# Gate fold, norm sums, first weight sums and final norm of a two-layer decoder trunk: work moved between engines and places

## The chip, the cores and the metric

The kernel runs on one core of a Trainium2 chip. A core has a matrix engine (TensorE, PE in the profile), a vector engine (VectorE, DVE), an activation engine (ScalarE, ACT), a general engine (GpSimd, POOL), and a queue engine (SyncE, SP) that issues most of the transfers. The metric is the device time of one execution in microseconds (us).

## The reference

The model is a trunk of two layers on 1024 tokens of width 1024, in float32. Cut to what matters here:

```
def rmsnorm(x, g):
    y = x * rsqrt(mean(x * x, -1) + EPS)
    return y * g

# layer 0
h = rmsnorm(x, g_mix[0])
x = x + gla_layer_mix(h, mem_k, mem_v, ...)        # gated linear attention beside memory attention
x = x + conv_ffn(rmsnorm(x, g_ffn[0]), w_up[0], conv_w[0], conv_b[0], w_down[0])
# keys and values of sparse attention, made once
shared = nsa_shared_kv(x, g_kv, w_kv, ...)
# layer 1
h = rmsnorm(x, g_mix[1])
q, gl, mq = split_cols(h @ w_in, [512, 24, 512])
gates = sigmoid(gl)                                # 24 per token: 8 heads x 3 branches
m = mem_attend(mq, mem_k, mem_v)                   # 4 heads over 256 memory tokens
x = x + concat(nsa_attend(q, gates, *shared), m) @ w_out
x = x + conv_ffn(rmsnorm(x, g_ffn[1]), w_up[1], ...)
return rmsnorm(x, g_final)

def conv_ffn(h, w_up, conv_w, conv_b, w_down):
    a, b = split(h @ w_up, 2)                      # w_up: 1024 x 5632, so 22 tiles of 128 columns each
    a = causal conv of width 3 over time(a) + conv_b
    return (silu(a) * b) @ w_down
```

## The kernel before

Activations lie transposed: 8 tiles `xs[k]` of 128 features by 1024 tokens, worked in two halves of 512 tokens. TensorE takes a float32 product as three passes over values split in two: a rounded high part and the rest (low part), high x high, high x low, low x high. So each operand is split first: ScalarE copies the high part (`Ah`, line 979), VectorE subtracts it from the source for the low part (`Al`, line 980). The program is recorded in the order of the Python code, generators woven by weights, and a list scheduler then sets each engine's order from the dependences and its own costs; buffers come from pools by tag (`U` gives 128x512 buffers, `V` 128x1024).

**Feed-forward, up part.** Each layer has 22 units (`Up`), one for each tile of columns. A unit loads its weights (`load`, two tiles `wu` of 128x1024), and makes seven products p1 to p7 of combined weights with combined activations `B[1]` to `B[7]` (a seven-product scheme in place of eight). p1 and p2 need the raw weights; p6 and p7 (PSUM tile `fy`), p3 and p5 (`fw`) need sums of them, which `sums()` makes in place by four 128x512 operations at lines 999 to 1002, all on GpSimd; then `split67` and `split35` split them. The list `seq` begins with the units us[0] and us[1] (worked as a pair), then us[6], us[2] and so on. The combined activations come from `blocks0` and `blocks1` (lines 553 to 586 are their VectorE operations), behind the norm of the attention's result. While VectorE is at that, ScalarE and VectorE also split the raw weights of the first units (`pre`, `direct`).

**Norms.** `Norm.add` squares a tile on ScalarE (`nsq`, line 256) and adds it into one of two running sums `nacc` (line 266): the first sum on GpSimd, the second on VectorE, in the output projections of the two attention stages (`out_proj`); all on VectorE elsewhere. `done` adds the two sums (line 274), lets TensorE sum over the features (`ms`, line 278), and calls `inv_rms`: logarithm and exponential on ScalarE give a first value y of the inverse root, and one Newton step of four VectorE operations (lines 241 to 244) refines it, y(1.5 - 0.5 (ms + eps) y y).

**Gates.** In layer 1, `front` makes the keys to be compressed (`comp_in`, for each of two kinds one VectorE operation, eight ScalarE copies `ck`, and in the second half two additions at line 1465) and the 24 gates of each token (`gsb`, line 1479) for one half of the tokens after the other. High and low contributions of a gate stand in two rows, so eight small matmuls with a 0/1 matrix `fold` (`gateT`, line 1497) add them and turn them to tokens; three small operations (lines 1499 to 1501, tile `ope`) start the sigmoid. This stands ahead of the memory attention: `mkv.project()` (TensorE `mk`, lines 192 to 194, over four weights whose low parts are `wmkl`, line 177, and then the sums `mms`, line 353), and with it `compress()` (`hid`, line 1536).

**End.** The down part of the feed-forward (`dn`, lines 1341 to 1343) adds its products to `x` on VectorE (line 1389, or line 1306 when it leaves PSUM into scaled sums). In layer 1 its output comes in three segments: 512 tokens, 256, 256 (the third and fourth quarters). For each, `finish` takes the norm and scales 8 tiles with the gain and the inverse root: six by one VectorE operation (line 1830), two (k = 1 and 4) by GpSimd (line 1827) and ScalarE (line 1828), and stores two or four tiles at a time (SyncE). `after_ffn1` weaves the three `finish` generators with what is left of the down part (`d`).

The lines that set the order around the change:

```
weave((front(0), 14.0), (second, 9.0))          # gates and compressed keys of the first half
drain(front(1))                                  # of the second half
... fold, gateT, ope                             # lines 1492 to 1501
weave((mem_all(), 107.0), (compress(), 15.0))

def after_ffn1(d, nn, segs):
    drain(take(d, 5))
    weave((finish(segs[0], nn[0]), 9.0), (take(d, 10), 27.0))
    drain(take(d, 4 + 4))
    weave((finish(segs[1], nn[1]), 9.0), (take(d, 4), 3.6))
    drain(finish(segs[2], nn[2]))
```

Of the kernel before, what the change touches and what calls it, by code (L numbers as in the profile page):

```python
# [10 lines left out]
AF = mybir.ActivationFunctionType  # L11
# [3 lines left out]
P = 128  # L15
# [3 lines left out]
HT = 512  # L19
# [15 lines left out]
def kernel(  # L35
# [46 lines left out]
    def PS(s="ps"):  # L82
        return pp.tile([P, HT], F32, tag="ps", name=nm(s))
# [22 lines left out]
    def weave(*gens):  # L106
        drain(blend(*gens))
# [43 lines left out]
    def col(c):  # L151
        return cs[:, c : c + 1]
# [83 lines left out]
    def inv_rms(ms, n, y=None, a=None):  # L236
        y = U(s="rs") if y is None else y
        a = U(s="rt") if a is None else a
        nc.scalar.activation(a[:, :n], ms, AF.Ln, bias=epsc)
        nc.scalar.activation(y[:, :n], a[:, :n], AF.Exp, scale=-0.5)  # L240
        nc.vector.scalar_tensor_tensor(a[:, :n], ms, EPS, y[:, :n], ALU.add, ALU.mult)
        nc.vector.tensor_tensor(a[:, :n], a[:, :n], y[:, :n], ALU.mult)
        nc.vector.tensor_scalar(a[:, :n], a[:, :n], -0.5, 1.5, ALU.mult, ALU.add)
        nc.vector.tensor_tensor(y[:, :n], y[:, :n], a[:, :n], ALU.mult)
        return y

    class Norm:
        def __init__(self, width=HT, pool=True):
            self.eng = (nc.gpsimd if pool else nc.vector, nc.vector)
            self.acc = [None, None]  # L250
            self.n = 0
            self.w = width
# [6 lines left out]
        def add(self, xt):  # L259
            j = self.n % 2  # L260
            self.n += 1
            if self.acc[j] is None:
                self.acc[j] = self.square(xt, "nacc")
            else:
                sq = self.square(xt, "nsq")
                self.eng[j].tensor_tensor(self.acc[j], self.acc[j], sq, ALU.add)

        def add_last(self, xt):
            self.acc.append(self.square(xt, "nsq"))
# [335 lines left out]
    def mix_a():  # L605
# [3 lines left out]
        last_x = [None]  # L609

        def stats(half, h=None):
            n = Norm(pool=False)
            tvs = []
            for k2 in range(4):
                t = V(s="x0")
# [324 lines left out]
    def ffn(l, blocks_, after):  # L940
        B, rest = blocks_
        segs = [(0, HT), (HT, HT)]
        ends = segs if l == 0 else [(0, HT), (HT, HT // 2), (HT + HT // 2, HT // 2)]
        nn = [Norm(w, False) for _, w in ends]
        silu = [None]

        ring = {}
# [18 lines left out]
        class Up:  # L966
# [28 lines left out]

            def sums(self):
                (a0, b0), (a1, b1) = ((t[:, hs(0)], t[:, hs(1)]) for t in self.raw)
                tt = nc.gpsimd.tensor_tensor
                tt(b1, b0, b1, ALU.add)  # L999
                tt(b0, a0, b0, ALU.subtract)  # L1000
                tt(a0, b1, a0, ALU.subtract)
                tt(a1, a1, a0, ALU.subtract)
# [124 lines left out]
        def each(group, *whats):  # L1127
            for what in whats:
                for u in group:
                    getattr(u, what)()  # L1130
# [37 lines left out]
        seq = pair + order[:-1]  # L1168
        for n, u in enumerate(seq):
            u.n, u.mate = n // 2, seq[n - 1] if n % 2 else None  # L1170
        each(pair, "load", "direct")
        each(pair, "p1")
        pair[0].p2()
# [258 lines left out]
    def mix_b(second, h, rs, rst):  # L1432
# [58 lines left out]
        fold = cp.tile([64, 24], F32, name="fold")  # L1491
        nc.vector.tensor_tensor(fold, ident[0:64, 0:24], ident[0:64, 32:56], ALU.add)
        ope = cp.tile([P, 8, 24], F32, name="ope")
        pg = PS("gateT")
        for qt in range(8):
            t = gsb[qt // 4][0:64, (qt % 4) * P : (qt % 4 + 1) * P]
            mm(pg[:, qt * 24 : (qt + 1) * 24], t, fold, start=True, stop=True)
        opf = ope.rearrange("p a b -> p (a b)")
        nc.vector.tensor_scalar(opf, pg[:, :192], -87.0, None, ALU.max)
        nc.scalar.activation(opf, opf, AF.Exp, scale=-1.0)  # L1500
        nc.vector.tensor_scalar(opf, opf, 1.0, None, ALU.add)

        hid = [S([P, 2, P], s="state", bufs=2) for i in range(2)]

        rows = [slice(0, 64), slice(64, 128)]
# [45 lines left out]
            yield from att.rest()  # L1551

        weave((mem_all(), 107.0), (compress(), 15.0))

        kcr = [S([P, 2, P], F32R, s="state", bufs=2) for _ in range(2)]
        vc = S([P, P], s="vcmp", bufs=1)
# [257 lines left out]
            weave(*gens)  # L1814
        return second_half(op0, b_wo, x_d, nn, C_FFN + 8)

    def finish(seg, nrm):
        t0, w = seg
        rs = nrm.done()[:, :w]
        per = 2 * HT // w  # L1820
        for k in range(KT):
            if k % per == 0:
                o = V(s="fin")
            ov = o[:, (k % per) * w : (k % per + 1) * w]
            xv = xs[k][:, t0 : t0 + w]
            if k in (1, 4):
                nc.gpsimd.tensor_tensor(ov, xv, rs, ALU.mult)
                nc.scalar.activation(ov, ov, AF.Copy, scale=col(C_FIN + k))
            else:
                nc.vector.scalar_tensor_tensor(ov, xv, col(C_FIN + k), rs, ALU.mult, ALU.mult)  # L1830
            if k % per == per - 1:
                nc.sync.dma_start(
                    out[k + 1 - per : k + 1, :, t0 : t0 + w].rearrange("k p t -> p k t"),
                    o[:, : per * w].rearrange("p (k t) -> p k t", k=per),
                )
            yield 1.0

    def after_ffn1(d, nn, segs):
        drain(take(d, 5))
        weave((finish(segs[0], nn[0]), 9.0), (take(d, 10), 27.0))  # L1840
        drain(take(d, 4 + 4))
        weave((finish(segs[1], nn[1]), 9.0), (take(d, 4), 3.6))
        drain(finish(segs[2], nn[2]))

    b = ffn(0, mix_a(), after_ffn0)
    ffn(1, mix_b(*b), after_ffn1)
# [102 lines left out]
```

## Time and profile before

| what | value |
|---|---|
| three timed runs | 2336.86, 2341.9, 2342.29 us; median 2341.9 us |
| profiled execution | 2342.82 us, of which the span is 2341.0 us |
| mean granted clock of TensorE in it | 0.991 of full speed |
| TensorE busy | 2264.1 us, 97% |
| VectorE busy | 1743.6 us, 74% |
| ScalarE busy | 1130.0 us, 48% |
| GpSimd busy | 442.2 us, 19% |

The profiled execution is 1.8 us longer than its span: that much lies around the span. TensorE's matmuls are pipelined, so one is shown longer (0.39 us for 128x512) than the step from one start to the next. A granted clock of 0.50 is the lower of the two levels of TensorE's clock, 1.2 GHz, and 1.00 the higher, 2.4 GHz. The names of buffers in the rows stand without their numbers; `fy<-B,Ah` is a matmul from activations `B` and high parts `Ah` into `fy`.

### The profile page before, as it was taken

The numbers are of one execution on the slowest core, as the hardware profiler recorded it, in microseconds if no ns is written. First come the engines' busy times: TensorE is split into PE (matmuls) and PEld (weight loads), VectorE is DVE, ScalarE is ACT, GpSimd is POOL, SyncE is SP. The second block draws the span as 40 slices with busy tenths as digits, with TensorE's granted clock in tenths as the row PEclk, the third lists the DMA queues.
The fourth block names the chain that finished last, engine by engine and source line by source line (L and its number), as shares of the span: only waits on it lengthen the run. The fifth ranks groups of instructions, "written<-read, shape, count | busy, mean of one in ns | idle before, by whom it ended". The sixth has DMA issues, their size and how long they took to land.

```text
span 2341.0 us, 31315 instructions
## 1 busy us (share of the span) xinstructions
PE 2264.1 (97%) x11062; PEld 1842.3 (79%) x11062; DVE 1743.6 (74%) x3065; ACT 1130.0 (48%) x2054; POOL 442.2 (19%) x383
## 2 busy tenths in 40 slices
PE   8999999999999999999899999999999999999997
PEld 6888777777888888788787877767777788888886
DVE  6785876977876668886656688884978777768876
ACT  5463454533333335456444688773543333335454
POOL 1211301323333200000002121110323422210001
PEclk9999999999999999999999999999999999999999
DMA  6233146433432329542421111027434433229533
GB/s 216 93 109 101 54 144 202 135 112 122 140 122 95 108 98 330 167 131 105 126 89 37 45 44 35 8 61 225 136 108 135 140 104 108 95 87 338 165 96 102
DMA packets 138892, 284.94 MB, mean 122 GB/s; under 512 B 16086, under 2 KB 22403, under 8 KB 138736
## 3 DMA queue, kind: packets, MB, share of 16 engines
q1 hardware_dynamic: 130144, 262.20, 34.4%
q0 software_dynamic: 3840, 12.24, 1.5%
q10 hardware_dynamic: 4752, 8.51, 1.0%
q8 instruction: 86, 1.41, 0.3%
q14 instruction: 70, 0.57, 0.1%
HBM read 211.06 MB, written 71.83 MB: 121 GB/s over the span
## 4 chain that ended last, share of the span: by engine, by line
PE 75%; DVE 13%; DMA 4%; ACT 3%; issue 3%; POOL 1%; SPq 1%; DVEq 0%; POOLq 0%; ACTq 0%
PE dn L1342 5%; PE dn L1341 5%; PE dn L1343 5%; PE fy L1017 5%; PE fy L1015 4%; PE fy L1016 4%; PE no L1753 3%; PE fw L1017 3%; PE fw L1016 3%; PE fw L1015 3%; PE npt L1737 2%; PE fx L1015 2%; PE fx L1016 2%; PE fx L1017 2%; PE sc L1680 2%
## 5 line engine op out<-in xcount | busy, mean ns | idle before, releaser
L1341 PE MATMUL dn<-db,da 128*128 128x512 f32 (+1 forms) x628 | 242.8, 387 | 2.1 <-DVE x L1306 2.1
L1342 PE MATMUL dn<-db,da 128*128 128x512 f32 (+1 forms) x628 | 242.6, 387 | 1.0 <-DVE db L1271 1.0
L1343 PE MATMUL dn<-db,da 128*128 128x512 f32 (+1 forms) x628 | 242.2, 386 | 0.0
L1015 PE MATMUL fy<-B,Ah 128*128 128x512 f32 x496 | 197.0, 397 | 16.7 <-DVE q L1049 8.7
L1017 PE MATMUL fy<-B,Al 128*128 128x512 f32 x496 | 195.9, 395 | 1.7 <-DVE Al L980 1.4
L1016 PE MATMUL fy<-B,Ah 128*128 128x512 f32 x496 | 195.3, 394 | 0.0
L979 ACT ACTIVATE Ah<-wu 128x1024 fp32r<-128x1024 f32 x124 | 130.3, 1052 | 106.6 <-PE fy L1016 61.7
L980 DVE TENSOR_TENSOR Al<-wu,Ah 128x1024 fp32r<-128x1024 f32 x124 | 161.6, 1304 | 20.8 <-ACT Ah L979 20.8
L999 POOL TENSOR_TENSOR wu<-wu,wu 128x512 f32<-128x512 f32 x44 | 61.3, 1394 | 558.7 <-DVE Al L980 320.6
L1341 PEld LDWEIGHTS dn<-db,da 128*128 128x128 f32 x628 | 118.1, 188 | 26.6 <-issue 2.8
L1342 PEld LDWEIGHTS dn<-db,da 128*128 128x128 f32 x628 | 118.0, 188 | 26.2 <-DVE db L1271 2.8
L1017 PE MATMUL fw<-B,Al 128*128 128x512 f32 x352 | 137.9, 392 | 0.0
L1016 PE MATMUL fw<-B,Ah 128*128 128x512 f32 x352 | 137.2, 390 | 0.0
L1015 PE MATMUL fw<-B,Ah 128*128 128x512 f32 x352 | 137.1, 390 | 0.0
L1343 PEld LDWEIGHTS dn<-db,da 128*128 128x128 f32 x628 | 118.0, 188 | 23.5
L1271 DVE TENSOR_TENSOR db<-bl,db 128x512 fp32r<-128x512 f32 x154 | 107.6, 699 | 31.3 <-ACT db L1270 30.4
L1015 PEld LDWEIGHTS fy<-B,Ah 128*128 128x128 f32 x496 | 94.2, 190 | 41.8 <-DVE q L1049 12.9
L1017 PEld LDWEIGHTS fy<-B,Al 128*128 128x128 f32 x496 | 94.2, 190 | 23.8 <-DVE Al L980 4.0
L1270 ACT ACTIVATE db<-bl 128x512 fp32r<-128x512 f32 x154 | 95.6, 622 | 30.3 <-PE dn L1343 21.8
L1016 PEld LDWEIGHTS fy<-B,Ah 128*128 128x128 f32 x496 | 94.3, 190 | 19.2
L192 PE MATMUL op<-om,wor 128*128 128x512 f32 x256 | 103.0, 404 | 1.9 <-ACT om L224 1.9
L1270 ACT ACTIVATE da<-wb 128x512 fp32r<-128x512 f32 x88 | 55.1, 629 | 98.4 <-PE dn L1342 61.3
(424 smaller groups left out, 6239.6 us busy)
## 6 DMA issues: line engine op xcount, KB each, us to landing
wu<-in_w_up_dram SPq DMA_DIRECT2D x176, 256.0 KB, 3.0
bl<-gb_d SPq DMA_DIRECT2D x154, 256.0 KB, 2.8
gb_d<-fc SPq DMA_DIRECT2D x132, 256.0 KB, 3.0
wb<-in_w_down_dram SPq DMA_DIRECT2D x44, 256.0 KB, 4.6
wa<-in_w_down_dram SPq DMA_DIRECT2D x22, 512.0 KB, 7.8
wo<-in_a_wo_dram SPq DMA_DIRECT2D x16, 512.0 KB, 3.7
xre<-om_d SPq DMA_DIRECT2D x32, 256.0 KB, 5.1
x_r<-x SPq DMA_DIRECT2D x32, 256.0 KB, 2.4
```

The source lines that it names most:

```text
L192: mm(ps, wr[:, k, :], hr, start=(k == 0), stop=False)
L979: a = nc.scalar.activation(hi, src, AF.Copy)
L980: b = nc.vector.tensor_tensor(lo, src, f(hi), ALU.subtract)
L1015: mm(ps, wr, hr, start=(first and j == 0), stop=False, skip_group_check=True)
L1016: mm(ps, wr, hl, start=False, stop=False, skip_group_check=True)
L1017: mm(ps, wl, hr, start=False, stop=(stop and j == 3), skip_group_check=True)
L1270: nc.scalar.activation(w[:, hs(0)], t, AF.Copy)
L1271: b = tt(w[:, hs(1)], t, f(w)[:, hs(0)], ALU.subtract)
L1341: mm(o, hi, bh, start=first, stop=False, skip_group_check=True)
L1342: mm(o, hi, bl, start=False, stop=False, skip_group_check=True)
L1343: mm(o, lo, bh, start=False, stop=stop or n == NP - 1, skip_group_check=True)
L1753: mm(acc[a * 64 : a * 64 + 64, :256], v, pf[:, a * 256 : (a + 1) * 256], start=(n == 0), stop=(n == last[a]),)
```

## The change

1. `inv_rms`: y y comes from a ScalarE `Square`; VectorE has three operations in place of four.
2. `Norm.add`: every addition is on VectorE.
3. `sums()` of the first four units of each layer (us[0], us[1], us[6], us[2]) is on VectorE, that of the other 18 stays on GpSimd.
4. The gates' fold with its three small operations is recorded behind the memory attention and `compress`, ahead of the compressed keys' product.
5. `finish` gets the inverse root as an argument; the 512-token segment is scaled by VectorE alone; in the two quarters ScalarE multiplies by the gain, which doesn't need the norm, and VectorE multiplies four tiles at a time by the inverse root. `after_ffn1` takes the norms of both quarters before either is scaled.

```diff
@@ inv_rms
-        nc.vector.scalar_tensor_tensor(a[:, :n], ms, EPS, y[:, :n], ALU.add, ALU.mult)
-        nc.vector.tensor_tensor(a[:, :n], a[:, :n], y[:, :n], ALU.mult)
+        nc.scalar.activation(a[:, :n], y[:, :n], AF.Square)
+        nc.vector.scalar_tensor_tensor(a[:, :n], ms, EPS, a[:, :n], ALU.add, ALU.mult)
         nc.vector.tensor_scalar(a[:, :n], a[:, :n], -0.5, 1.5, ALU.mult, ALU.add)
         nc.vector.tensor_tensor(y[:, :n], y[:, :n], a[:, :n], ALU.mult)
@@ Norm.add
-                self.eng[j].tensor_tensor(self.acc[j], self.acc[j], sq, ALU.add)
+                nc.vector.tensor_tensor(self.acc[j], self.acc[j], sq, ALU.add)
@@ Up.sums
-                tt = nc.gpsimd.tensor_tensor
+                tt = (nc.vector if self.soon else nc.gpsimd).tensor_tensor
@@ ffn
             u.n, u.mate = n // 2, seq[n - 1] if n % 2 else None
+            u.soon = n < 4
@@ mix_b
-        pg = PS("gateT")
-        for qt in range(8):
...
-        nc.vector.tensor_scalar(opf, opf, 1.0, None, ALU.add)
-
         hid = [S([P, 2, P], s="state", bufs=2) for i in range(2)]
...
         weave((mem_all(), 107.0), (compress(), 15.0))
+
+        pg = PS("gateT")
+        for qt in range(8):
+            t = gsb[qt // 4][0:64, (qt % 4) * P : (qt % 4 + 1) * P]
+            mm(pg[:, qt * 24 : (qt + 1) * 24], t, fold, start=True, stop=True)
+        opf = ope.rearrange("p a b -> p (a b)")
+        nc.vector.tensor_scalar(opf, pg[:, :192], -87.0, None, ALU.max)
+        nc.scalar.activation(opf, opf, AF.Exp, scale=-1.0)
+        nc.vector.tensor_scalar(opf, opf, 1.0, None, ALU.add)
@@ finish, after_ffn1
-    def finish(seg, nrm):
+    def finish(seg, rs):
         t0, w = seg
-        rs = nrm.done()[:, :w]
...
-            if k in (1, 4):
-                nc.gpsimd.tensor_tensor(ov, xv, rs, ALU.mult)
-                nc.scalar.activation(ov, ov, AF.Copy, scale=col(C_FIN + k))
+            if per == 2:
+                nc.vector.scalar_tensor_tensor(ov, xv, col(C_FIN + k), rs, ALU.mult, ALU.mult)
             else:
-                nc.vector.scalar_tensor_tensor(ov, xv, col(C_FIN + k), rs, ALU.mult, ALU.mult)
+                nc.scalar.activation(ov, xv, AF.Copy, scale=col(C_FIN + k))
             if k % per == per - 1:
+                o3 = o.rearrange("p (k t) -> p k t", k=per)
+                if per > 2:
+                    nc.vector.tensor_tensor(o3, o3, rs.unsqueeze(1).broadcast_to([P, per, w]), ALU.mult)
...
     def after_ffn1(d, nn, segs):
-        drain(take(d, 5))
-        weave((finish(segs[0], nn[0]), 9.0), (take(d, 10), 27.0))
-        drain(take(d, 4 + 4))
-        weave((finish(segs[1], nn[1]), 9.0), (take(d, 4), 3.6))
-        drain(finish(segs[2], nn[2]))
+        drain(take(d, 11))
+
+        def first():
+            yield from finish(segs[0], nn[0].done())
+
+        weave((first(), 9.0), (take(d, 8), 21.6))
+        drain(take(d, 4 + 3))
+        r1 = nn[1].done()[:, : segs[1][1]]
+        drain(d)
+        r2 = nn[2].done()[:, : segs[2][1]]
+        drain(finish(segs[1], r1))
+        drain(finish(segs[2], r2))
```

What this does to the order is shown at three places.

GpSimd before, at the sums of the third and fourth unit of layer 0 (us[6] has the tiles `wu_3507` and `wu_3508`, us[2] `wu_3505` and `wu_3506`):

```order
L999 TENSOR_TENSOR wu_3506<-wu_3505,wu_3506 128x512
L1000 TENSOR_TENSOR wu_3505<-wu_3505 128x512
L1001 TENSOR_TENSOR wu_3505<-wu_3506,wu_3505 128x512
L1002 TENSOR_TENSOR wu_3506<-wu_3506,wu_3505 128x512
L999 TENSOR_TENSOR wu_3508<-wu_3507,wu_3508 128x512
L1000 TENSOR_TENSOR wu_3507<-wu_3507 128x512
L1001 TENSOR_TENSOR wu_3507<-wu_3508,wu_3507 128x512
L1002 TENSOR_TENSOR wu_3508<-wu_3508,wu_3507 128x512
```

VectorE before, in the same stretch; `Al_3809` is the low part that the third unit's p6 needs:

```order
L1064 TENSOR_TENSOR fc_3575<-fc_3575,s_648_3544 128x512
L980 TENSOR_TENSOR Al_3524<-wu_3508,Ah_3523 128x1024
L1063 TENSOR_TENSOR s_650_3559<-fy_3831,s_650_3559 128x512
L1064 TENSOR_TENSOR fc_3604<-fc_3604,s_650_3559 128x512
L1069 TENSOR_TENSOR q_3829<-fw_3900,q_3829 128x512
L980 TENSOR_TENSOR Al_3809<-wu_3507,Ah_3808 128x1024
L1069 TENSOR_TENSOR q_3844<-fw_3914,q_3844 128x512
L980 TENSOR_TENSOR A_3518<-wu_3507,A_3518 128x512
```

VectorE in the changed kernel, in the same stretch:

```order
L1062 TENSOR_TENSOR s_650_3559<-fy_3831,s_650_3559 128x512
L998 TENSOR_TENSOR wu_3508<-wu_3507,wu_3508 128x512
L1063 TENSOR_TENSOR fc_3604<-fc_3604,s_650_3559 128x512
L999 TENSOR_TENSOR wu_3507<-wu_3507 128x512
L1068 TENSOR_TENSOR q_3829<-fw_3900,q_3829 128x512
L1000 TENSOR_TENSOR wu_3507<-wu_3508,wu_3507 128x512
L998 TENSOR_TENSOR wu_3506<-wu_3505,wu_3506 128x512
L1001 TENSOR_TENSOR wu_3508<-wu_3508,wu_3507 128x512
L979 TENSOR_TENSOR Al_3809<-wu_3507,Ah_3808 128x1024
L1068 TENSOR_TENSOR q_3844<-fw_3914,q_3844 128x512
L999 TENSOR_TENSOR wu_3505<-wu_3505 128x512
L1000 TENSOR_TENSOR wu_3505<-wu_3506,wu_3505 128x512
```

The eight sums have gone from GpSimd to VectorE, and those of the third unit, which stood behind those of the fourth, now stand ahead of three of them; the low part `Al_3809` comes after five sums.

TensorE before, at the gates' fold (`gsb_8390` holds the gates of the first half of the tokens, `gsb_8538` those of the second; the `mk` around are those of the first memory weight):

```order
L193 MATMUL mk_8579<-mh_8432,wmkr_8580 128x256
L194 MATMUL mk_8579<-mh_8432,wmkl_8581 128x256
L1497 MATMUL gateT_8557<-fold,gsb_8538 128x24 x4
L192 MATMUL mk_8579<-mh_8437,wmkr_8580 128x256
L193 MATMUL mk_8579<-mh_8437,wmkr_8580 128x256
L194 MATMUL mk_8579<-mh_8437,wmkl_8581 128x256
```

TensorE in the changed kernel, in the same place; the first weight's `mk` run without a break:

```order
L192 MATMUL mk_8567<-mh_8432,wmkr_8568 128x256
L193 MATMUL mk_8567<-mh_8432,wmkr_8568 128x256
L194 MATMUL mk_8567<-mh_8432,wmkl_8569 128x256
L192 MATMUL mk_8567<-mh_8437,wmkr_8568 128x256
L193 MATMUL mk_8567<-mh_8437,wmkr_8568 128x256
```

TensorE in the changed kernel, some 640 rows later, where the fold now stands:

```order
L472 MATMUL mo_9732<-mpT_9721,mV_8805 128x512
L1549 MATMUL gateT_9742<-fold,gsb_8390 128x24 x4
L1549 MATMUL gateT_9742<-fold,gsb_8538 128x24 x2
L473 MATMUL mo_9732<-mpT_9721,mV_8805 128x512
L471 MATMUL mo_9732<-mpT_9729,mV_8808 128x512
L472 MATMUL mo_9732<-mpT_9729,mV_8808 128x512
L473 MATMUL mo_9732<-mpT_9729,mV_8808 128x512
L1549 MATMUL gateT_9742<-fold,gsb_8538 128x24 x2
```

The fold of the second half no longer stands between the `mk` of the first weight; both halves' fold stands among the last products of the memory attention (`mo`) and ahead of the compressed keys' product.

VectorE before, at the end of the program (the four `x` tiles of the last quarter's second block are done one by one; `rs_18975` is the third quarter's inverse root, `rs_19052` the fourth's):

```order
L1389 TENSOR_TENSOR x_17731<-dn_18518,x_17731 128x256
L1830 SCALAR_TENSOR_TENSOR fin_18983<-x_17727,cs,rs_18975 128x256
L1830 SCALAR_TENSOR_TENSOR fin_18983<-x_17731,cs,rs_18975 128x256
L266 TENSOR_TENSOR nacc_18755<-nacc_18755,nsq_19011 128x256
L1830 SCALAR_TENSOR_TENSOR fin_18983<-x_17733,cs,rs_18975 128x256
L266 TENSOR_TENSOR nacc_18747<-nacc_18747,nsq_19029 128x256
L1830 SCALAR_TENSOR_TENSOR fin_19016<-x_17497,cs,rs_18975 128x256
L1830 SCALAR_TENSOR_TENSOR fin_19016<-x_17499,cs,rs_18975 128x256
L1830 SCALAR_TENSOR_TENSOR fin_19016<-x_17501,cs,rs_18975 128x256
L1389 TENSOR_TENSOR x_17733<-dn_18519,x_17733 128x256
L241 SCALAR_TENSOR_TENSOR rt_19053<-ms_19048,rs_19052 128x256
L242 TENSOR_TENSOR rt_19053<-rt_19053,rs_19052 128x256
```

VectorE in the changed kernel, at the end:

```order
L265 TENSOR_TENSOR nacc_18724<-nacc_18724,nsq_19005 128x256
L1389 TENSOR_TENSOR x_17733<-dn_18519,x_17733 128x256
L242 SCALAR_TENSOR_TENSOR rt_19013<-ms_19008,rt_19013 128x256
L243 TENSOR_SCALAR rt_19013<-rt_19013 128x256
L244 TENSOR_TENSOR rs_19012<-rs_19012,rt_19013 128x256
L1832 TENSOR_TENSOR fin_19044<-fin_19044,rs_19012 128x1024
L242 SCALAR_TENSOR_TENSOR rt_19037<-ms_19032,rt_19037 128x256
L1832 TENSOR_TENSOR fin_19051<-fin_19051,rs_19012 128x1024
L243 TENSOR_SCALAR rt_19037<-rt_19037 128x256
L244 TENSOR_TENSOR rs_19036<-rs_19036,rt_19037 128x256
L1832 TENSOR_TENSOR fin_19058<-fin_19058,rs_19036 128x1024
L1832 TENSOR_TENSOR fin_19065<-fin_19065,rs_19036 128x1024
```

The scalings of the third quarter stood ahead of the last addition to `x`; now every addition stands ahead of them, the fourth quarter's norm is refined between them, and there are four scalings of 128x1024 in place of 12 of 128x256.

## Rows read from the trace of the kernel before

**Rows 1.** The page, part 1: busy time, share and instructions of each engine.

```profile
PE 2264.1 (97%) x11062; PEld 1842.3 (79%) x11062; DVE 1743.6 (74%) x3065; ACT 1130.0 (48%) x2054; POOL 442.2 (19%) x383
```

**Rows 2.** TensorE's waits: releaser; us in total, times, longest us.

```profile
PE gateT L1497 <- DVE gsb L1479: 8.2, 1, 8.2
PE fy L1015 <- ACT Ah L979: 8.0, 4, 4.0
...
PE gr L194 <- DVE wrl L177: 2.5, 1, 2.5
...
PE ms L278 <- DVE nacc L274: 2.2, 2, 1.3
...
PE dn L1341 <- DVE x L1306: 2.1, 1, 2.1
```

**Rows 3.** Windows: us, PE, PEld, DVE, ACT, POOL busy; PEclk, DMA, GB/s.

```profile
504.00:506.00 2.00, 1.88 (x5) 0.97 (x5) 1.48 (x2) 0.00 (x0) 0.00 (x0) 0.50 0.08 9
...
1130.00:1132.00 2.00, 2.00 (x14) 2.00 (x13) 1.21 (x4) 1.06 (x1) 0.00 (x0) 0.65 0.50 90
...
80.00:100.00 20.00, 17.51 (x96) 14.86 (x95) 18.57 (x21) 11.26 (x14) 7.26 (x4) 1.00 0.24 69
440.00:460.00 20.00, 18.50 (x78) 14.42 (x78) 19.82 (x28) 10.13 (x17) 5.73 (x4) 1.00 0.24 89
```

**Rows 4.** TensorE's timeline at the third unit: start, us, instruction, idle before.

```profile
503.59 0.80 PE L1015 MATMUL fy<-B,Ah 128*128 128x512 f32 x1 [3.97 <-ACT Ah L979]
...
510.20 0.39 PE L1017 MATMUL fx<-B,Al 128*128 128x512 f32 x1
...
1742.76 0.80 PE L1015 MATMUL fy<-B,Ah 128*128 128x512 f32 x1 [3.57 <-ACT Ah L979]
```

**Rows 5.** Timeline of GpSimd and ScalarE ahead of it.

```profile
491.56 1.67 POOL L999 TENSOR_TENSOR wu<-wu,wu 128x512 f32<-128x512 f32 x1 [45.59 <-DVE A L980]
...
501.19 1.26 POOL L1001 TENSOR_TENSOR wu<-wu,wu 128x512 f32<-128x512 f32 x1
...
502.48 1.06 ACT L979 ACTIVATE Ah<-wu 128x1024 fp32r<-128x1024 f32 x1 [10.78 <-POOL wu L1001]
```

**Rows 6.** VectorE's timeline at the start of the feed-forward, layer 0.

```profile
427.95 1.22 DVE L980 TENSOR_TENSOR Al<-wu,Ah 128x1024 fp32r<-128x1024 f32 x1
...
437.77 1.78 DVE L266 TENSOR_TENSOR nacc<-nacc,nsq 128x512 f32<-128x512 f32 x1
...
463.39 2.49 DVE L225 TENSOR_TENSOR B<-x,B 128x512 fp32r<-128x512 f32 x4
```

**Rows 7.** VectorE's lines from 426 to 447 us: busy us, mean ns, idle before.

```profile
L980 DVE TENSOR_TENSOR Al<-wa,Ah 128x1024 fp32r<-128x1024 f32 x4 | 8.1, 2033 | 2.4 <-ACT Ah L979 2.4
```

**Rows 8.** Timeline of three engines at the gates' fold.

```profile
1092.27 0.91 ACT L227 ACTIVATE mh<-mem,cs 128x256 fp32r<-128x256 f32 x2 [3.67 <-DMA mem<-in_mem_dram]
...
1125.93 1.90 PE L1497 MATMUL gateT<-fold,gsb 64*128 64x24 f32 x8 [8.17 <-DVE gsb L1479]
...
1128.75 1.22 DVE L177 TENSOR_TENSOR wmkl<-wmk,wmkr 128x1024 fp32r<-128x1024 f32 x1
...
1138.46 0.59 PE L353 MATMUL mms<-macc,on_d 128*128 128x256 f32 x2
```

**Rows 9.** Timeline of the end.

```profile
2283.36 3.50 POOL L1827 TENSOR_TENSOR fin<-x,rs 128x512 f32<-128x512 f32 x2 [206.18 <-DVE rs L244]
...
2324.55 0.28 PE L1342 MATMUL dn<-db,da 128*128 128x256 f32 x1
2324.67 0.28 PE L1343 MATMUL dn<-db,da 128*128 128x256 f32 x1
2327.45 1.13 PE L278 MATMUL ms<-nacc,on_d 128*128 128x256 f32 x4 [2.50 <-DVE nacc L266]
...
2328.50 0.41 DVE L1389 TENSOR_TENSOR x<-dn,x 128x256 f32<-128x256 f32 x1
...
2333.32 3.40 DVE L1830 SCALAR_TENSOR_TENSOR fin<-x,cs,rs 128x256 f32<-128x256 f32 x6
```

More of the change, by code (lines that the diff above doesn't have):

```diff
@@ L247, with __init__ @@
     class Norm:
-        def __init__(self, width=HT, pool=True):
-            self.eng = (nc.gpsimd if pool else nc.vector, nc.vector)
+        def __init__(self, width=HT):
             self.acc = [None, None]
@@ L611, in stats @@
         def stats(half, h=None):
-            n = Norm(pool=False)
+            n = Norm()
             tvs = []
@@ L943, in ffn @@
         ends = segs if l == 0 else [(0, HT), (HT, HT // 2), (HT + HT // 2, HT // 2)]
-        nn = [Norm(w, False) for _, w in ends]
+        nn = [Norm(w) for _, w in ends]
         silu = [None]
@@ L1493, in mix_b @@
         ope = cp.tile([P, 8, 24], F32, name="ope")
-        pg = PS("gateT")
-        for qt in range(8):
[L1496 to L1500, printed above, removed]
-        nc.vector.tensor_scalar(opf, opf, 1.0, None, ALU.add)
         hid = [S([P, 2, P], s="state", bufs=2) for i in range(2)]
@@ L1825, in finish @@
             xv = xs[k][:, t0 : t0 + w]
-            if k in (1, 4):
-                nc.gpsimd.tensor_tensor(ov, xv, rs, ALU.mult)
-                nc.scalar.activation(ov, ov, AF.Copy, scale=col(C_FIN + k))
+            if per == 2:
+                nc.vector.scalar_tensor_tensor(ov, xv, col(C_FIN + k), rs, ALU.mult, ALU.mult)
             else:
-                nc.vector.scalar_tensor_tensor(ov, xv, col(C_FIN + k), rs, ALU.mult, ALU.mult)
+                nc.scalar.activation(ov, xv, AF.Copy, scale=col(C_FIN + k))
             if k % per == per - 1:
[L1832 to L1835, printed above, removed]
+                o3 = o.rearrange("p (k t) -> p k t", k=per)
+                if per > 2:
+                    nc.vector.tensor_tensor(o3, o3, rs.unsqueeze(1).broadcast_to([P, per, w]), ALU.mult)
+                nc.sync.dma_start(out[k + 1 - per : k + 1, :, t0 : t0 + w].rearrange("k p t -> p k t"), o3)
             yield 1.0
     def after_ffn1(d, nn, segs):
-        drain(take(d, 5))
-        weave((finish(segs[0], nn[0]), 9.0), (take(d, 10), 27.0))
-        drain(take(d, 4 + 4))
-        weave((finish(segs[1], nn[1]), 9.0), (take(d, 4), 3.6))
-        drain(finish(segs[2], nn[2]))
+        drain(take(d, 11))
[8 more added lines that the diff above has]
+        drain(finish(segs[2], r2))
     b = ffn(0, mix_a(), after_ffn0)
```

## The prediction

> **What bounds the kernel now.** The page comes first: TensorE is busy 97% of the span, so about 77 us of the whole are its idle time, and VectorE follows at 74% [rows 1]. A change on the other engines can therefore only give back waits of TensorE, or what a wait costs behind its end; 0.3% is 7 us, about what a measurement of this kernel can tell from no change. So the next view is TensorE's waits, and there I look for the lines that the diff touches. Five of them are there: the gates' fold waits 8.2 us in one piece, p6 waits 8.0 us for the high parts `Ah`, the norm's matmul 2.2 us for the sums of squares, the down product 2.1 us for `x` [rows 2], and the last norm 2.5 us [rows 9].
>
> The third view is the windows, for the granted clock. The two p6 waits are 3.97 and 3.57 us [rows 4], and behind the first the clock stands at 0.50, 1.2 GHz; behind the fold's wait it is 0.65 as late as 1130 to 1132 [rows 3]. Where TensorE waited 2.5 us for another low part (`gr` [rows 2], between 80 and 100 us) the clock stayed at 1.00 [rows 3]. So the long waits cost twice. Between the p6 at 503.59 and the matmul at 510.20 there are 14 matmuls; at the full clock they step by 0.227 us, 3.2 us in all, and they took 6.6: 3.4 us lost [rows 4]. I take the same for layer 1.
>
> **A, the fold.** Removed are 8.2 us of waiting and the low clock from 1125.93 to about 1131.4 (0.65 in the last window is 1.4 us of two at half rate), 5.5 us at half rate, 2.7 us lost. But something else is late next. Ahead of the sums `mms` TensorE needs the low part of the third memory weight, which VectorE began at 1128.75 and had at 1129.97 [rows 8]. In the changed order the compressed keys' copies stand ahead of the memory's on ScalarE, which idled 3.67 us for the memory's transfer at 1092 [rows 8]; I estimate that the second half's chain (norm, keys, third weight) moves up by 2 to 3 us through that and through the three small operations that are gone, so the third low part is there at 1127.0. TensorE, no longer held, has 24 `mk`, 16 `hid` and 24 more `mk` from 1115.1 on, 0.12 us each as the steps of that size at the end [rows 9], some 7.9 us: it arrives at 1123.0 and waits 4.0. Then 24 more, and `mms` begins at 1130.7 if the clock holds, at 1132.3 if it falls, in place of 1138.46 [rows 8]: 7.8 or 6.2 us. The fold itself is paid later, at most 1.1 us (the eight small matmuls; the first four ran ahead without a wait). I take 6. Bounds: if the third weight is no earlier, 3; if the fold hides in a wait of the memory attention and the clock holds, 8.
>
> The Trainium skill's page "TensorE: Matmul & The Clock Gate", Part 1, says that the throttled clock is the default and activity releases it. By that the new 4 us of idle time would bring the low clock back, and A would be the 6.2 less 1.1; the trace agrees at 3.57 and 3.97 us of waiting. The sum does not hang on it, as 5.1 lies inside the bounds above.
>
> **B, the start of both feed-forwards.** The third unit's p6 waited since GpSimd did the fourth unit's sums first: it began at 491.56 and reached the third unit's third sum at 501.19, and ScalarE's `Ah` followed at 502.48 [rows 5]. In the new order VectorE does the third unit's sums first. A 128x512 operation of two tensors takes it 0.62 us (2.49 over four [rows 6]). From 491.4 it has two low parts (1.8 us), three operations on TensorE's results and three sums (3.7 us), so ScalarE can begin `Ah` near 497 and has it by 498.9 at the latest, ahead of TensorE's arrival at 499.6 (503.59 less 3.97 [rows 4]). Both p6 waits go, with their low clock: 3.97 + 3.57 + 2 x 3.4 = 14.3 us.
>
> VectorE pays eight sums more (5.0 us) and about three additions of squares (1.9 us) in the stretch from 426 to 469, where it is already full: 19.82 of 20 us [rows 3]. One Newton operation, 0.7, goes. Against these 6.2 us stands what GpSimd's presence costs it now: four low parts there took 8.1 us [rows 7] where an undisturbed one takes 1.22 [rows 6], 3.2 us too much; the addition at 437.77 took 1.78 in place of 0.62 [rows 6], and three more operations lose 0.8 each by my estimate, 6.8 in all. So the stretch comes out even or 0.6 shorter, and the norm's wait of 2.2 us [rows 2] goes with the slow additions. That makes 14.3 + 2.2 = 16.5; I take off 0.5 for waits of a few tenths that move: 16. Bounds: 17.5 if small waits for the low parts go as well, 8 if VectorE is the late one at p6 and the clock falls all the same, so that only part of the wait and the 2.2 come back.
>
> **C, the down product.** Its 2.1 us wait for `x` [rows 2] lies where GpSimd's scaling of the first segment (two operations, 3.50 us at 2283.36 [rows 9]) runs beside VectorE. The scaling now starts later in the down part, and GpSimd has none. I take 1.9; bounds 0 and 2.1.
>
> **D, the end.** The last matmul begins at 2324.67, but the last addition to `x` only at 2328.50, behind the third quarter's scalings; from there to the end of the span are 12.5 us [rows 9]. In the new order nothing of that stands ahead of it. ScalarE is the limit then: 16 gain copies and the squares, some 0.42 each by my estimate, and the last square is about 2.2 us earlier than it was. Behind it the norm has one ScalarE operation more and one VectorE operation fewer (even), and the last six scalings of 3.40 us [rows 9] become two of 1.2, one of the third quarter's ahead of the last ones: 0.2 better. I take 2.4, bounds 0.5 (ScalarE's queue eats it) and 4 (all of the 3.5 us that the addition waited, and the shorter scalings).
>
> **E, small losses.** Every norm has a `Square` more on ScalarE, in layer 0's feed-forward behind a table load; 12 additions of squares come to VectorE; the two gate tiles hold 2 of 14 buffers through the memory attention. I take 1.3 us of loss in all, bounds 0 and 4; cover is ScalarE's half-idle time and VectorE's quarter [rows 1].
>
> **Sum.** 6 + 16 + 1.9 + 2.4 - 1.3 = 25.0 us off the profiled execution of 2342.8 gives 2317.8. The median of the runs is 0.9 below the profiled one, so the forecast is 2317.
>
> **Rivals.** *More comes back* (2310): every term at its upper bound, 8 + 17.5 + 2.1 + 4 and no loss, is 31.6. For it: VectorE without GpSimd beside it may be ahead everywhere. Against it: A has a new wait whose end I can name.
>
> *The waits at p6 change their name* (2329): VectorE, with five sums ahead of `Al`, is late at p6 by 2 to 4 us, and the low clock stays. Then B is 8 and E doubles to 2.6 while C and D hold: 6 + 8 + 1.9 + 2.4 - 2.6 = 15.7, or 2326; with A at its lower bound, 2329. For it: 19.82 of 20 us [rows 3]. Against it: VectorE is idle ahead of p6 now, and the sums fit there.
>
> *Nothing comes of it* (2340): each wait removed meets one that is as late, as a transfer of weights behind the sums would be. Against it: `Ah` waited 10.78 us for GpSimd's sum and for nothing else [rows 5].
>
> *Slower* (2350): VectorE's long durations at 426 to 447 are its own and not GpSimd's doing. Then 6.2 us come on top of a full engine in each layer, the activations `B` are late by as much, and TensorE waits 6 us at p6 and runs at half rate for 3.4 more, twice: 18.8 us lost, the third unit's 14.3 us not gained, and A, C and D give 10.3 back: 8.5 slower. It decides from about 2 us of backlog per layer on, if the clock falls with it. Against it: the same low part takes 1.22 and 2.03 within the one stretch [rows 6, 7], and GpSimd's own sums took 1.67 beside VectorE and 1.26 when that was idle [rows 5].
>
> **Chances.** The forecast with A to E inside their bounds, 2311 to 2325, has 0.60; more comes back 0.15; the waits change their name 0.15; nothing 0.06; slower 0.04. The range from 2308 to 2333 takes in the first three with little of the edges lost. All three are faster by over 0.3%, less 0.02 for a weak third case: 0.88. Within 0.3% 0.07, slower 0.05 with 0.01 for mishaps in E.
>
> **What would show it.** In the changed profile the `fy` line has no wait over 1 us for `Ah`, and the clock is 1.00 behind the third unit's p6 in both layers; `gateT` waits for nothing; a new wait of 3 to 5 us stands at `mk` for `wmkl` near 1123 to 1127; the low parts at the start of the feed-forward take 1.2 us each; the last addition to `x` follows the last matmul within 1 us. The prediction is wrong if the windows behind p6 still show 0.50, if VectorE's stretch from the attention's end to the third unit has grown, or if the last square starts no earlier behind the last matmul than 4 us.

## The result

| | us |
|---|---|
| kernel before, six runs | 2336.86 to 2343.62, median 2340.22 |
| changed kernel, six runs | 2315.2 to 2322.32, median 2318.12 |
| forecast, range | 2317, 2308 to 2333 |
| ratio, 95% interval | 0.9902, 0.9887 to 0.9917 |
| profiled executions: spans | 2341.0 before, 2313.7 after |

The kernel became faster by 22.1 us in the medians, 0.9%, where 25 were forecast. The sum held; its terms did not hold alike. The profiled execution of before is one of its longer ones and that of after one of the shorter, so the two traces lie 27.3 us apart.

### The profile page after: what moved, and what is told of

It reads as the page before. It is cut to its first block, busy times and chain, and to the rows that moved or that the text cites. A ratio compares the mean times of both kernels' runs of the same rounds, so it can differ in the third digit from the quotient of the medians.

```text
span 2313.7 us, 31260 instructions
## 1 busy us (share of the span) xinstructions
PE 2256.4 (98%) x11062; PEld 1839.1 (79%) x11062; DVE 1735.4 (75%) x3086; ACT 1139.0 (49%) x2081; POOL 365.4 (16%) x333
## 3 DMA queue, kind: packets, MB, share of 16 engines
q8 instruction: 87, 1.43, 0.3%
## 4 chain that ended last, share of the span: by engine, by line
PE 84%; DVE 7%; DMA 4%; ACT 3%; issue 2%; SPq 1%; POOL 0%; DVEq 0%; ACTq 0%; POOLq 0%
PE dn L1342 5%; PE dn L1341 5%; PE dn L1343 5%; PE fy L1014 5%; PE fy L1016 4%; PE fy L1015 4%; PE fx L1014 3%; PE no L1753 3%; PE fx L1015 3%; PE fx L1016 3%; PE fw L1016 3%; PE fw L1015 3%; PE fw L1014 3%; PE npt L1737 2%; PE op L193 2%; PE op L192 2%
## 5 line engine op out<-in xcount | busy, mean ns | idle before, releaser
L978 ACT ACTIVATE Ah<-wu 128x1024 fp32r<-128x1024 f32 x124 | 130.4, 1052 | 100.9 <-PE fy L1015 60.3
L998 POOL TENSOR_TENSOR wu<-wu,wu 128x512 f32<-128x512 f32 x36 | 49.3, 1369 | 744.4 <-DVE Al L979 410.6
L1014 PEld LDWEIGHTS fy<-B,Ah 128*128 128x128 f32 x496 | 93.4, 188 | 36.3 <-DVE q L1048 10.4
```

The costliest lines, as they stand in the source:

```text
L978: a = nc.scalar.activation(hi, src, AF.Copy)
L1014: mm(ps, wr, hr, start=(first and j == 0), stop=False, skip_group_check=True)
```

## The profile after

The first view is again the page, then TensorE's waits (releaser; us in total, times, longest us).

```profile
PE 2256.4 (98%) x11062; PEld 1839.1 (79%) x11062; DVE 1735.4 (75%) x3086; ACT 1139.0 (49%) x2081; POOL 365.4 (16%) x333
```

```profile
PE fy L1014 <- DVE q L1048: 6.6, 7, 1.4
PE mk L194 <- DVE wmkl L177: 5.0, 1, 5.0
PE fy L1014 <- ACT Ah L978: 4.7, 3, 2.7
```

The reader is to see what is gone and what is new. The lines of `gateT`, of `ms` for VectorE's sums and of `dn` for `x` [rows 2] are gone. The line of `fy` for `Ah` has fallen from 8.0 to 4.7 us only, and a line of 5.0 us for `wmkl` has come. The line of `fy` for `q`, VectorE's operation on the result of a unit's p6, was 8.7 us before and is 6.6; no part of the change is aimed at it.

**At the third unit** ScalarE's timeline now reads:

```profile
497.73 1.06 ACT L978 ACTIVATE Ah<-wu 128x1024 fp32r<-128x1024 f32 x1 [6.48 <-DVE wu L1000]
```

`Ah` starts at 497.73 in place of 502.48 [rows 5]; p6 starts at 499.96 without a wait in place of 503.59 [rows 4]. The windows of after (us, PE, PEld, DVE, ACT, POOL busy, PEclk, DMA, GB/s) show the clock behind it, in layer 0 and in layer 1, and then a place where it did fall:

```profile
500.00:502.00 2.00, 2.00 (x10) 1.65 (x9) 1.94 (x4) 1.55 (x2) 0.00 (x0) 1.00 0.45 120
...
1726.00:1728.00 2.00, 2.00 (x10) 1.65 (x10) 1.74 (x3) 1.37 (x3) 0.00 (x0) 1.00 0.79 262
...
514.00:516.00 2.00, 2.00 (x7) 1.56 (x7) 2.00 (x5) 0.63 (x1) 0.00 (x0) 0.62 0.00 0
516.00:518.00 2.00, 2.00 (x7) 1.57 (x6) 2.00 (x4) 0.00 (x0) 0.00 (x0) 0.53 0.49 137
```

The low clock of 0.50 at p6 is gone [rows 3]. In layer 0 the next unit's p6 waits. Its `Ah` on ScalarE stands behind the split of the weights of the unit after it, and that one waits for those weights, whose transfer (first row, from SyncE's timeline) was issued only behind VectorE's low part of 504.55 to 505.77, the last to read that buffer:

```profile
506.21 0.42 SPq L975 DMA_DIRECT2D wu<-in_w_up_dram  x1
...
510.63 1.06 ACT L978 ACTIVATE Ah<-wu 128x1024 fp32r<-128x1024 f32 x1 [2.77 <-DMA wu<-in_w_up_dram]
...
513.72 0.50 PE L1014 MATMUL fy<-B,Ah 128*128 128x512 f32 x1 [2.72 <-ACT Ah L978]
```

In the kernel before, the same split at 514.90 waited for nothing: TensorE was up to 7 us later there, and ScalarE came to this split behind other work. This is a wait that the prediction did not have; in layer 1 it is 1.1 us.

**At the start of the feed-forward** VectorE's low parts are no longer stretched (line; busy us, mean ns; idle before), where the mean was 2033 ns [rows 7]:

```profile
L979 DVE TENSOR_TENSOR Al<-wa,Ah 128x1024 fp32r<-128x1024 f32 x4 | 4.9, 1220 | 2.2 <-ACT Ah L978 2.2
```

**At the gates' old place** TensorE no longer waits for `gsb`, but for the third memory weight; its row, and those of VectorE ahead of it:

```profile
1121.54 1.22 DVE L1465 TENSOR_TENSOR ck<-ck,pe 128x1024 f32<-128x1024 f32 x1 [0.81 <-ACT ck L1459]
...
1123.01 1.22 DVE L177 TENSOR_TENSOR wmkl<-wmk,wmkr 128x1024 fp32r<-128x1024 f32 x1
...
1124.29 0.58 PE L194 MATMUL mk<-mh,wmkl 128*128 128x256 f32 x1 [4.99 <-DVE wmkl L177]
```

The low part's source on ScalarE had been ready since 1114.3; VectorE came to it at 1123.01 because two additions `ck` stood ahead of it in its order and waited for ScalarE's copies. The clock fell to 0.50 again (0.51 from 1122 to 1124); `mms` starts at 1129.02.

**At the fold's new place**, ahead of the compressed keys' product `kcmp`, the fold's matmuls now take time of TensorE that is not idle otherwise, the row below and 0.62 us more from 1255.13 on (the trace has two records for each of the eight):

```profile
1252.57 1.51 PE L1549 MATMUL gateT<-fold,gsb 64*128 64x24 f32 x12
```

**At the end**, from the last matmul of the down part on:

```profile
2300.68 0.28 PE L1343 MATMUL dn<-db,da 128*128 128x256 f32 x1
...
2301.00 0.42 DVE L1389 TENSOR_TENSOR x<-dn,x 128x256 f32<-128x256 f32 x1 [1.03 <-PE dn L1343]
...
2302.45 0.70 PE L277 MATMUL ms<-nsq,on_d 128*128 128x256 f32 x2 [0.62 <-ACT nsq L255]
```

The last addition follows the last matmul after 0.3 us, where it took 3.8 [rows 9]; from that matmul to the end of the span are 13.0 us in place of 16.3.

Where the time went is best seen by stage. The borders are the first starts of matmuls into named tiles (`op` of the second half of the tokens, the norm `ms` behind the first feed-forward, `mms`, `kcmp`, which is the compressed keys' product, `fx` and `dn` of the second feed-forward), read off each trace; the table has the time between them in us.

| execution | feed-forward 0 | to `mms` | to `kcmp` | sparse attention | feed-forward 1 up | down and end |
|---|---|---|---|---|---|---|
| before | 682.4 | 64.3 | 124.9 | 408.2 | 438.2 | 231.2 |
| after | 678.3 | 58.4 | 126.7 | 405.0 | 427.8 | 225.3 |
| the whole change again (below) | 675.4 | 58.0 | 129.3 | 405.4 | 427.5 | 225.5 |
| the fold alone | 684.3 | 60.3 | 128.0 | 407.7 | 435.5 | 233.0 |
| the sums alone | 672.3 | 64.2 | 124.0 | 406.8 | 430.4 | 231.7 |
| the end alone | 681.8 | 63.7 | 123.9 | 406.0 | 435.0 | 225.3 |
| the square alone | 679.2 | 63.3 | 125.1 | 405.5 | 436.2 | 231.0 |

Stages that an edit does not touch differ by 2 to 3 us between executions (408.2 and 438.2 of before are the highest of their columns), so one cell tells no more than that.

## The experiments

Ratios are to the kernel before, run beside each kernel, with 95% intervals. Between these sets of runs the median of before itself moved between 2338.46 and 2341.89. The edits are cut to the lines that tell them apart; the remarks behind # in them are added.

**The fold alone.** The code of `gateT` and `ope` moved, nothing else.

```diff
-        pg = PS("gateT")            # eight matmuls and three operations, ahead of hid
+        pg = PS("gateT")            # the same, behind weave((mem_all(), 107.0), (compress(), 15.0))
```

> Only part 4 of the change: the gates' fold behind the memory attention. If the fold's wait and the low clock behind it were the cost and the third weight's low part is late next, 4 to 7 us faster than the kernel before, with a wait of 4 to 6 us at mk for wmkl and no wait at gateT. If the low part's chain is what sets the time anyway (rival), within 2 us of before. If the compressed keys' copies moved by another part of the change made the gain, no gain here.

Measured 0.9996 (0.9982 to 1.001): nothing. TensorE's waits there:

```profile
PE mk L194 <- DVE wmkl L177: 6.5, 2, 5.4
```

The third low part started at 1128.95, as late as before [rows 8]. The sums `mms` began 4.0 us sooner behind the norm even so (60.3 in place of 64.3), but 3.1 of this were given back up to `kcmp`, where the fold's matmuls now take 2.4 us. So the time is that of the rival; its reason, that the late low part sets the time anyway, holds for part of it only.

**The sums alone.** Part 3.

```diff
-                tt = nc.gpsimd.tensor_tensor
+                tt = (nc.vector if self.soon else nc.gpsimd).tensor_tensor
```

> Only part 3: the sums of the first four units of each layer on VectorE. If the waits at the third unit's p6 were GpSimd's doing, 10 to 16 us faster, no wait over 1 us for Ah at p6 and no low clock behind it. If VectorE's long operations at the start of the feed-forwards are its own (rival), slower by some 8 us, with the low parts there still at 2.0 us. If the norm's additions must leave GpSimd as well for VectorE to be in time, less than 8 us.

Measured 0.9938 (0.9919 to 0.9957), 14.4 us in the medians: the first theory. By the stages it is 10.1 us in layer 0 and 7.8 in layer 1, the latter less the 2 to 3 us by which other kernels without the sums lie below before. The low parts took 1.5 us on mean and not 2.0, though there is more on VectorE.

**The end alone.** Part 5 (`finish` and `after_ffn1` as in the change).

```diff
-    def finish(seg, nrm):
+    def finish(seg, rs):            # and after_ffn1 as in the change
```

> Only part 5: the final norm and its order. By the terms of the prediction for the down product's wait and the end, 4.3 us faster (0.5 to 6). By the two traces, in which the distance between before and after grows by some 6 us from the down part to the end, 6 us. If that growth is owed to other parts (rival), under 2 us.

Measured 0.9966 (0.9954 to 0.9978), 8.3 us. In the trace 231.2 became 225.3, of which 3.3 lie behind the last matmul (13.0 us there too). These 5.9 us lie inside the interval; what the medians show beyond them falls on no stage that the edit touches.

**The norm's parts.** Parts 1 and 2.

```diff
-            self.eng = (nc.gpsimd if pool else nc.vector, nc.vector)
+            self.eng = (nc.vector, nc.vector)   # and the square on ScalarE in inv_rms
```

> Only parts 1 and 2: the Newton step's square on ScalarE, all additions of squares on VectorE. Alone these take 1 to 3 us off (the norm's wait of 2.2 us over two layers), or nothing if GpSimd's sums still stretch the same operations; the rival is a loss of 1 to 3 us, since 12 additions come to a full VectorE.

Measured 0.9980 (0.9969 to 0.9992), 3.8 us: more than forecast, by a side effect. The fold's wait fell to 6.7 us, as the compressed keys' copies stand ahead of the memory's on ScalarE in this kernel.

**The square alone**, to tell which of the two parts did that.

```diff
-        nc.vector.tensor_tensor(a[:, :n], a[:, :n], y[:, :n], ALU.mult)
+        nc.scalar.activation(a[:, :n], y[:, :n], AF.Square)   # ahead of the operation with eps
```

> Part 1 alone (the square on ScalarE in each norm). If this part is what puts the compressed keys' copies ahead of the memory's on ScalarE and moves the chain at 1090 to 1130 us up: 1 to 3 us faster with the gateT wait at 6 to 7 us. If the additions of squares are (rival), nothing, with that wait at 8 us.

Measured 0.9967 (0.9955 to 0.9979), with the `gateT` wait at 6.7 us: part 1 is what moves the chain. The third low part begins 53.1 us behind the norm, where it was 54.5 before. ScalarE's timeline there, where before it waited 3.67 us for the memory [rows 8]:

```profile
1093.79 0.63 ACT L1459 ACTIVATE ck<-kcs 64x248 f32<-64x248 f32 x1
1094.44 1.71 ACT L227 ACTIVATE mh<-mem,cs 128x256 fp32r<-128x256 f32 x4
```

Part 1 alone is no slower than parts 1 and 2 together, so the additions of squares on VectorE gave nothing that shows; alone they were not run. The 6.7 us in the medians are more than the 1.5 us by which the chain moved; where the rest lies is not shown.

**All but the fold.** Parts 1, 2, 3 and 5.

```diff
-        weave((mem_all(), 107.0), (compress(), 15.0))   # of the change: gateT behind it
+        pg = PS("gateT")                                # back ahead of hid
```

> The whole change without part 4 (the fold stays ahead of the memory attention). The fold alone gave nothing, since the third memory weight's low part was then as late as before (it began at 1128.95 us there, 1128.75 before), and the norm parts moved that chain up by 3 us by themselves. If the fold is worth something only together with that earlier chain: 2 to 4 us slower than the whole change (ratio 0.991 to 0.992 to the kernel before), with a wait of 6 to 7 us at gateT. If the fold is worth nothing at all (rival): the same as the whole change, 0.9902. If it is worth the 6 us of the prediction: 0.9927 or more.

Measured 0.9904 (0.9888 to 0.9919), the whole change's ratio. TensorE waited at the fold instead:

```profile
PE gateT L1498 <- DVE gsb L1480: 6.6, 1, 6.6
```

To `kcmp` it took 62.7 and 123.8 us, 186.5 in all, against 185.1 and 187.3 in the two executions of the whole change. So the fold's move is worth less than the intervals, some 3 us, can tell; 6 is excluded only weakly by this run, as the whole change itself gave 0.9902 and 0.9883 in two sets of runs, but by the fold alone as well.

**GpSimd's order only.** The kernel before; the fourth unit's sums stand behind the third's, all on GpSimd.

```diff
+                op = tt(b1, b0, b1, ALU.add)
+                if self is us[2]:
+                    follow(op, us[PRE].summed, "order")
```

> The kernel before with one edit: GpSimd keeps all sums, but in each layer the fourth unit's stand behind the third unit's. If the order of GpSimd's work was the cost, the wait at the third unit's p6 goes with its low clock and this gives 10 to 14 us, nearly what part 3 gave (14.4). If GpSimd's slowness is the cost (rival), the third unit's sums, which begin near 493.5 us and take 1.3 to 2.2 each, are late all the same, and this gives under 5 us.

Measured 0.9964 (0.9952 to 0.9977), 7.3 us: between the two. The long wait and the low clock went, as the window behind p6 shows, but waits of 0.6 to 1.2 us for `s`, `Al` and `Ah` came, as GpSimd's sums were still slower, and PE is not full:

```profile
500.00:502.00 2.00, 1.52 (x7) 1.26 (x8) 1.02 (x2) 0.00 (x0) 1.92 (x2) 1.00 0.17 45
```

Moving the same two units' sums to VectorE (the next run, beside the same runs of before) gave 12.0. So a good half of that is the order of the two units, and the rest the engine.

**The third and fourth unit's sums only.** Part 3 with `n in (2, 3)`.

```diff
+            u.soon = n in (2, 3)
```

> Part 3 cut to the third and fourth unit of each layer; the first two units' sums stay on GpSimd beside VectorE's full stretch. If the p6 waits are the whole of part 3's gain: 12 to 15 us as with all four. If the stretch at the start of the feed-forward matters by itself (VectorE's low parts at 2.0 us beside GpSimd): 3 to 6 us less than with all four, so 8 to 11.

Measured 0.9947 (0.9933 to 0.9962), 12.0 us. The first pair's sums stayed on GpSimd, and the low parts at the start as stretched as ever:

```profile
L980 DVE TENSOR_TENSOR Al<-wa,Ah 128x1024 fp32r<-128x1024 f32 x4 | 8.1, 2032 | 1.9 <-ACT Ah L979 1.9
```

The third and fourth unit's sums, and with them the waits at p6, are nearly all of the gain; VectorE's stretched operations are worth 2 us or nothing.

**The first segment on VectorE.** The kernel before, GpSimd out of the 512-token segment only.

```diff
-            if k in (1, 4):
+            if k in (1, 4) and per > 2:
```

> The kernel before with the 512-token segment of the final norm on VectorE alone, GpSimd kept in the two quarters and the order as it was. If GpSimd beside VectorE made the down product's wait of 2.1 us: 2 us faster, no such wait. If that wait is owed to the segment's place in the order (rival): no gain, and the wait stays or grows, since VectorE has two operations more there.

Measured 0.9983 (0.9971 to 0.9994), 4.4 us. The down product's wait for `x` is not among its waits any more, and the last stage took 229.7 us in place of 231.2: GpSimd beside VectorE was the cause of that wait, 1.5 to 2 us; the rest of the 4.4 falls on no stage that the edit touches.

**The third low part first.** The whole change, and the additions to the compressed keys of the second kind stand behind the third weight's low part and the memory's six sums.

```diff
+            if kind == 1:
+                follow(op, mkv.third, "order")
+                follow(op, mkv.summed, "order")
```

> The whole change, and VectorE does the third memory weight's low part and the six sums of the memory's squares ahead of the second kind's two additions to the compressed keys, which move behind them. If VectorE's order is what makes TensorE wait 5.0 us at mk for wmkl, that wait and the low clock behind it go, the sums mms start 4 to 7 us earlier in the stage, and the kernel is 3 to 6 us faster than the whole change (ratio 0.988 to 0.989). If the chain on ScalarE (the copies, the fourth weight) or the V weights' transfer takes over (rival), 0 to 2 us faster.

Measured 0.9880 (0.9867 to 0.9894), median 2312.23. The wait for the third low part is gone, and `mms` starts 51.2 us behind the norm in place of 58.4:

```profile
1118.80 0.59 PE L353 MATMUL mms<-macc,on_d 128*128 128x256 f32 x2
...
1121.07 0.39 PE L195 MATMUL mk<-mh,wmkl 128*128 128x256 f32 x1 [0.76 <-DVE wmkl L178]
```

But up to `kcmp` it took 130.3 us, 3.6 longer than in the changed kernel: half of the 7.2 us was given back inside the memory attention. Short waits for low parts make 1.0 of it (0.76 above and 0.27), and the clock an estimated 1.1: behind a wait of 1.43 us for ScalarE, right ahead of the fold, it fell here, and in the trace of the changed kernel, behind 1.44 us at the same place, it did not.

```profile
1248.00:1250.00 2.00, 2.00 (x10) 1.85 (x10) 0.39 (x2) 0.96 (x2) 0.00 (x0) 0.50 0.05 18
```

**The whole change again**, unaltered, and beside it **the third low part first, without the fold's move**:

```diff
-        pg = PS("gateT")            # behind the memory attention
+        pg = PS("gateT")            # back ahead of hid, with the additions still behind the low part
```

> The whole change, unaltered, beside the next run on the same chip: 0.989 to 0.992 of the kernel before, and no wait of 2.7 us for Ah near 513 us, if that wait was the accident of one execution (a weight tile that landed 4.3 us after its issue, where the median is 2.7). If it belongs to the change (rival), it is here again.

> The run in which VectorE does the third low part ahead of the second kind's additions, with the gates' fold left where it was before the change. If both waits, the fold's and the third low part's, have one cause, VectorE's order behind additions that wait for ScalarE's copies, the gates come early too and the fold costs its 1 to 2 us of small matmuls: 0.9875 to 0.989. If the fold must be moved for it (rival), its wait of 6 to 8 us is here again, and the time is that of the whole change or worse, 0.990 to 0.992.

The whole change gave 0.9883 (0.9869 to 0.9898), median 2315.58; without the fold's move and with the low part first it was 0.9881 (0.9866 to 0.9896), median 2313.81. In the first the wait for `Ah` in layer 0 is 1.3 us and not 2.7, in the second it is 2.6. So it belongs to the change, with a size that differs by execution; it was no accident. In the second the fold waits

```profile
PE gateT L1508 <- DVE gsb L1490: 3.4, 1, 3.4
```

half as long as where it stood behind the second kind's additions, though no wait was expected; the first kind's two additions are still ahead of the gates in VectorE's order. One cause, VectorE's order behind additions that wait for ScalarE's copies, lies under both waits. Whether the version with the low part first beats the changed kernel stays open: its median is the lowest of all, but the intervals 0.9867 to 0.9894 and 0.9869 to 0.9898 lie on one another.

## Why the prediction was right, point by point

**A, the fold: 6 forecast, nothing shown.** The mechanism was as written: the fold's wait went, a new one at `mk` for `wmkl` came (4.0 forecast, 5.0 measured), the clock fell in it, and `mms` started 5.9 us earlier against the 6.2 of the case with the low clock. The term that was mis-sized is the fold's price at its new place, 1.1 us at most: its matmuls take 2.0 and 2.8 us of TensorE's time there in the two executions of the whole change, and the part from `mms` to `kcmp` grew by 1.8 and 4.4. The earlier chain was right in size, 2.1 us (the third low part 52.4 us behind the norm, 54.5 before) against 2 to 3, but 1.5 of it were part 1's doing and came without the fold. What the move itself is worth is 0 in both runs that tell, with 3 us of uncertainty. The prediction named the late operation, the third low part on VectorE; that two additions held it up there was shown by the run that put it ahead of them. By the clock rule of the Trainium skill (its page "TensorE: Matmul & The Clock Gate", Part 1) that activity releases the throttle, the new wait would bring the low clock; the trace agrees, 0.51 in it and 0.50 behind it.

**B, both feed-forwards: 16 forecast.** The sums alone gave 14.4, and the run with the third and fourth unit's only 12.0; the p6 waits with their low clock, 14.3 in the sum, went in both layers as written. In the whole change layer 1 gave 10.4 to 10.7 us by the stages (other kernels without the sums lie 2 to 3 below before's 438.2, so 7 to 8 are its own), layer 0 only 4.1 and 7.0, where the sums alone gave 10.1. What the sum put at nothing is the next product: the fourth unit's p6 waits for its `Ah`, 2.7 and 1.3 us in layer 0 and 1.1 and 0.6 in layer 1, as ScalarE waits for the weights of the unit after it, and in the first execution the clock fell with the 2.7. That is not all, for the sums alone have the wait too, 1.2 in layer 0. Later units' p6 also wait for VectorE's `q`: from 520 us on in layer 0 for 4.3 us before, 3.6 and 5.7 in the whole change and 1.8 with the sums alone. Why that differs was not tested. That VectorE's stretch would come out even fits the runs and did not matter much, as the run with the third and fourth unit only shows.

**C and D, the end: 4.3 forecast**, 5.9 in the traces of after and of the end alone, 8.3 in the medians of the latter. C was right (the wait went, with GpSimd as the cause). D was too small: 3.3 behind the last matmul in place of 2.4, as the last norm's matmul starts 1.8 us behind the last down product's start (2302.45 less 2300.68), where its counterpart had waited for an addition that began only at 2328.50, 3.8 behind [rows 9]. The last square starts 1.3 behind that product in place of 4.3, 3.0 sooner where 2.2 were put: the gain copies on ScalarE cost less than allowed for.

**E, 1.3 of loss: wrong in sign for part 1.** The square on ScalarE alone made the kernel faster. No run has the other losses of this term alone.

Of the rivals, *the waits change their name* came true in part, in A and in layer 0, beside gains as large as forecast in layer 1 and at the end. *Slower* is excluded: the low parts fell from 2033 to 1220 ns when GpSimd left. Of the signs all held but the first: `fy` still waits over 1 us for `Ah`, in both layers, though no longer at the third unit. The parts taken alone (fold, sums, end, norm) add up to 26.5 us, and the whole gave 22.1 and 26.3 in two sets of runs, so no hindrance between them shows in the medians. That the sum met the result within 1.1 us owes something to luck, to errors that cancel: A too large, the end too small, a loss in E where part 1 gave a gain.

## What to carry to other kernels

Before a long wait is moved away, look what else stands behind the same instruction in that engine's queue: here an operation of VectorE that waited for ScalarE's copies held up the gates and the weights alike, and moving one waiter only let the next one wait. Where work is to go from a slow engine to a faster one, try its order on the slow one first: putting one unit's sums ahead of another's on the slow engine gave a good half of what a faster engine gave. An execution's stage table with an untouched stage beside it shows how much of a difference is the execution's own.

## What the runs showed of the hardware

A VectorE low part of 128x1024 took 1.22 us alone. Of the four behind the mean of 2.03 [rows 7] the first, before GpSimd's sums began, took 1.23, and the three beside them 2.28 to 2.31; the run with the third and fourth unit's sums only shows the same. GpSimd's 128x512 sums took 1.26 with VectorE idle and up to 2.28 beside it (the run with GpSimd's order only).

The length of a wait alone did not tell whether the clock would fall to its lower level behind it. A wait of 2.72 us was followed by granted clocks of 0.62 and 0.53 in the next two windows of 2 us, but one of 2.61 at the same p6, in the run with the low part first and the fold in its old place, by 1.00. The 2.5 us wait of `gr` was followed by 1.00 in the kernel before [rows 3] and by 0.55 and 0.60 in the whole change run again (windows from 98 to 102). The 1.4 us wait ahead of the compressed keys' product was followed by 1.00 in the first execution of the whole change and by 0.50 in the second and with the low part first. So the same program lost some us to the clock in one execution and not in another, which is part of why stages that no edit touched differ.
